# Moving one convolution pair of the input projection from the first part to the second, with its loads, scans and stores

## The chip, the cores and the metric

The kernel runs on one core of one Trainium2 chip. The metric is the device time of one execution in microseconds, the median over runs. The engines are TensorE (PE, with PEld for its weight loads), VectorE (DVE), ScalarE (ACT), GpSimd (POOL) and SyncE (SP). SP and POOL mostly issue DMAs here.

## What is computed

One layer of a decoder trunk on 1024 tokens of width 1024. The parts that matter, from the reference:

```python
h = rms_norm(x, g_mix[l])
z = jnp.einsum("bsd,de->bse", h, w_in[l]) + b_in[l]
va, ga, xb, gb, sa, sb = jnp.split(z, cuts, axis=-1)
u = va * jax.nn.sigmoid(ga)
u = causal_depthwise_conv(u, conv_a_w[l], conv_a_b[l])
...
v = causal_depthwise_conv(xb, conv_b_w[l], conv_b_b[l])
v = rg_lru(v, w_rg_a[l], b_rg_a[l], w_rg_x[l], b_rg_x[l], lam[l])
y_b = jnp.einsum("bsc,cd->bsd", v * jax.nn.gelu(gb), w_b_out[l])
```

After it come a layer norm, two more projections, gates, the output projection and an MLP, which the change doesn't touch. The projection `w_in` has 56 blocks of 128 columns: 8 of va, 8 of ga, 12 of xb, 12 of gb, 8 of sa and 8 of sb. A convolution over va times sigmoid(ga) has 31 taps; channel block j needs the column blocks VA + j and GA + j. `rg_lru` ends in a scan along the tokens.

## The kernel before

Matmuls take float32 operands as a high and a low part, each rounded for TensorE, and three products of these (high by high, high by low, low by high). A part is made in one of two ways: ScalarE copies the high part and VectorE subtracts it for the low one (`later(..., tensor_tensor, ..., ALU.subtract)`), or `split_dma` (L65 to L67) has ScalarE write the negated value, an accumulating DMA from POOL add the source, and ScalarE copy the high part.

**First part** (from L827, slots s = 3 to NC1 - 1, NC1 = 26). Each slot multiplies one column block of `w_in` (list `CH`) with all tokens: 24 pairs of operands times two halves, 48 matmuls (`chunk_mm`, L743). 16 head gates of `rg_lru` stand between, 12 matmuls each in two groups, the last at s = 22. The blocks are xb 0 to 11 and va, ga 0 to 6; the last two of `CH` are swapped. Beside it ScalarE and VectorE prepare the next weights (`w_parts`), gate the convolution input (`u_gate`, `u_mul`), and, three tiles at a time, run the scans: `scan_exp` (s = 22 for tiles 9 to 11), `scan_root` (s = 23, a square root with its own function table; it records a time `rooted[t]`), and `scan_tile` (L591), which takes a memset, three VectorE operations and a store of the tile to DRAM (`hd`, L597). Tile 9 goes in s = 23, tile 10 in s = 24, tile 11 in s = 25.

**Second part** (from L1038). The remaining 30 column blocks go in 15 pairs (`ZPAIRS`) by a seven-product scheme over 2 by 2 blocks (two columns by two halves of the rows; on the token side two token phases by the same halves). A product (i, p) is 12 matmuls (`z_mm`, L944). `zseq` orders them: pairs 0 and 1 are interleaved in 12 products, (0,1), (1,1), (0,2), (1,2), (0,6), (0,7), (1,7), (0,5), (1,6), (0,3), (0,4), (1,5), then seven for each pair. The left operand of product n + 4 is made in slot n (`z_lhs`, tile `zo`), sums of weight blocks it needs in slot n and n + 5 (`z_sums`, tile `zs`), and bank copies and results after the product (`z_post`, `z_post2`). Products p = 1, 2, 3 reuse the tokens of the first part; p = 6, 7, 5, 4 need differences of them, for each of two halves c2: `x_load` (L684) reads four tiles `xs` from DRAM, `x_sum` makes four differences on VectorE, and `x_parts` splits them into high and low (`xs6h`, `xs6l` and so on). The half c2 = 0 splits p = 5 and 4 by DMA, all others by VectorE. Each z product of p uses both halves.

A pair of gb columns is multiplied with the scan result (`z_h` loads `hd`, the product is stored to `hgd`); a pair with index below GA is a va, ga pair and goes to `z_u`, which makes the convolution input with a sigmoid; sa, sb pairs store gates. In the kernel before, pair 6 is va, ga 7.

**Order.** In these parts (`tc.manual_schedule`) ScalarE, VectorE, TensorE, SP and POOL run in the order of the code. VectorE's work of a slot is collected by `later(ready, cost, f, ...)` and emitted at the end of the slot by `vector_work`, sorted by `ready`, a time of the kernel's own cost clocks `clk`:

```python
    def vector_work(end):
        for ready, _, cost, f, a in sorted(todo, key=lambda x: x[:2]):
            dve(cost, ready, f, *a)
        todo.clear()
        taps["wait"] += fresh
        fresh.clear()
        fill(end)
```

`fill` puts taps of the convolutions (`conv`, L655, 47 operations each) where these clocks leave VectorE room. `ysum` collects the convolutions and is read by the layer norm after the second part. Most 128 by 1024 tiles come from one pool of 37 buffers (`T`). `z_load` (L761) brings a quarter of two pairs' weights into a pool "p" of 4 buffers, shared with the head inputs.

`XS` lists the token work by slot of the first part, `ZX` by product of the second. `x_load(1)` and the four `z_load`s of pairs 0 and 1 stand in slot NC1 - 3 = 23, in that order; `x_load(0)` in NC1 - 5 = 21.

Of the kernel before, what the change touches and what calls it, by code (L numbers as in the profile page):

```python
# [30 lines left out]
def trunk_kernel(ctx: ExitStack, tc: tile.TileContext, x, xt_in, xt_eo, vecs, w_in, w_a_out, w_b_pl, w_b_sq,  # L31
                 w_rg, w_o, w_1, w_2, g_final, out):

    nc = tc.nc
# [410 lines left out]
    VA, GA, XB, GB, SA, SB = 0, 8, 16, 28, 40, 48  # L445
# [72 lines left out]
    hd = dp.tile([12, P, S], F32, name="hd")  # L518
# [48 lines left out]
    at_, rooted = {}, {}  # L567
# [20 lines left out]
        for t in ts:  # L588
            later(ready, 1.2, nc.vector.tensor_tensor, gate[1, t], gate[1, t], vt.pop(t), ALU.mult)

    def scan_tile(t):  # L591
        a, r, i = at_.pop(t), gate.pop((0, t)), gate.pop((1, t))
        nc.vector.scalar_tensor_tensor(r, a, 1.0, r, ALU.add, ALU.mult)
        nc.vector.memset(r[:, 0:1], 1.0)
        nc.vector.tensor_tensor(i, r, i, ALU.mult)
        nc.vector.tensor_tensor_scan(i, a, i, 0.0, ALU.mult, ALU.add)  # L596
        nc.sync.dma_start(hd[t], i)  # L597

    ut = {}
    yd = dp.tile([8, P, S], F32, name="yd")  # L600
# [101 lines left out]
                      ALU.subtract)  # L702

    CH = [XB, VA, GA, XB + 1, XB + 2, VA + 1, GA + 1, XB + 3, XB + 4, XB + 5, VA + 2, GA + 2]
    CH += [XB + t for t in range(6, 12)] + [c for j in range(3, 7) for c in (VA + j, GA + j)]
    NU = 7
    CH[-2:] = CH[:-3:-1]
    NC1 = len(CH)
    zps = {n: z0[n] for n in range(N0)}
# [3 lines left out]
    def later(ready, cost, f, *a):  # L713

        todo.append((ready, len(todo), cost, f, a))
# [18 lines left out]
    def chunk_mm(s, n0, n1, halves=(0, 1)):  # L734

        wh, wl = wst[s]
        if s not in zps:
            zps[s] = PS(f"z{s}")
        pairs = [x for k in range(8) for x in ((wh, k, 0), (wh, k, 1))] + [(wl, k, 0) for k in range(8)]
        for n in range(n0, n1):  # L740
            w, k, part = pairs[n]
            for hf in halves:
                nc.tensor.matmul(zps[s][:, HALVES[hf]], w[:, k, :], xw[k][part][hf],  # L743
                                 start=n == 0, stop=n == 23)
        at("P", len(halves) * (n1 - n0) * MM)

    ZPAIRS = [GB + 2 * i for i in range(6)] + [VA + 7] + [SA + 2 * i for i in range(4)]
    ZPAIRS += [SB + 2 * i for i in range(4)]
    NZ = len(ZPAIRS)
    zraw, zs, zo, zb = {}, {}, {}, {}  # L750
    zn = [0]

    def z_load(i, kk):

        zraw[i, kk] = raw = qp.tile([P, 2, 4, P], F32, tag="p", name=f"zw{i}_{kk}", bufs=4)
        c = ZPAIRS[i]
        if c < GA:
            for m_, col in enumerate((GA + c, VA + c)):
                nc.sync.dma_start(raw[:, m_], w_in[col, :, 4 * kk:4 * kk + 4, :])
            return  # L760
        nc.sync.dma_start(raw, w_in[c:c + 2, :, 4 * kk:4 * kk + 4, :].rearrange("m p k c -> p m k c"))  # L761
# [47 lines left out]
    def z_get(n, f):  # L809
# [5 lines left out]
    head_at = {s: n for n, s in enumerate(HS0)}  # L815

    EXP = {head_slot: g for g, head_slot in enumerate(HS0[4 * g + 3] + 1 for g in range(4))}
    XS = {NC1 - 5: ((x_load, 0),), NC1 - 4: ((x_sum, 0),), NC1 - 3: ((x_load, 1), (x_parts, 0, 6)),
          NC1 - 2: ((x_sum, 1), (x_parts, 0, 7, 5)), NC1 - 1: ((x_parts, 0, 4), (x_parts, 1, 6))}
    made = []  # L820
    head_w(0)
    w_load(3)
# [4 lines left out]
    with tc.manual_schedule(engines=ENGINES):  # L827
        for s in range(3, NC1):
            w_load(s + 2)
            for t in sorted(vp_):  # L830
                head_load(t)
            taps["hold"] = False
            begun = clk["P"]
            clk["A"], clk["V"] = max(clk["A"], begun + 0.5), max(clk["V"], begun - 2)

            if s == 3:

                chunk_mm(s, 0, 24, (1,))
                rs = first_scale()
                first_product(0, rs)  # L840
                xb_out(0, zps[0])
                first_parts(rs)
                chunk_mm(s, 0, 24, (0,))
            else:
                mid = 16 if s - 1 in EXP else 12
                chunk_mm(s, 0, mid)
            before, new, nxt = (head_at.get(s + d) for d in (-1, 0, 1))
            if before is not None:

                head_gate(before, 0, begun)  # L850
                head_mm(before, 1)
            if made:
                xb_parts(made.pop())
            if s > 3:
                chunk_mm(s, mid, 24)
            if new is not None:
                head_mm(new, 0)

            c = CH[s - 1]
            if c >= XB:  # L860
                xb_out(c - XB, zps[s - 1])
            elif c >= GA:
                if CH[s] == c - GA + VA:
                    u_gate(c - GA, zps[s - 1])
                else:
                    u_out(c - GA, zps[s - 2], zps[s - 1])
            w_parts(s + 1)
            if before is not None:
                head_gate(before, 1, clk["P"] - (2 * (24 - mid) + 6) * MM)
            if s - 1 in EXP:  # L870

                scan_root(EXP[s - 1])
            if s == 3 or c >= XB:
                made.append(0 if s == 3 else c - XB)
            if nxt is not None:
                head_w_parts(nxt)
            if s in (5, 6):
                decay_on(27 if s == 5 else 99)
            if s + 2 in head_at:
                head_w(head_at[s + 2])  # L880

            def parts_now():
                if new is None and made:
                    vector_work(0)
                    xb_parts(made.pop())

            for d in range(5):
                if s - d in EXP:
                    g = EXP[s - d]
                    if d == 0:  # L890
                        scan_exp(g, parts_now)
                    if d == int(g < 3):
                        scan_in(begun if d else clk["P"] - 2, 3 * g, 3 * g + 1, 3 * g + 2)

                    t = 3 * g + d - (2 if g < 3 else 1)
                    if 3 * g <= t < 3 * g + 3:
                        later(rooted[t], 4.8, scan_tile, t)
            if s == NC1 - 1:
                z_get(0, z_lhs)
                z_get(1, z_lhs)  # L900
            for f, *a in XS.get(s, ()):
                f(*a)
            if s == NC1 - 3:
                for i in range(4):
                    z_load(i // 2, i % 2)
            if s == 3:
                for c2 in range(4):
                    nc.sync.dma_start(xu[0, c2], xc[c2])
            vector_work(clk["P"] - 0.7)
# [64 lines left out]
    def z_out(i, m_, hf, src, name):  # L974
        if ZPAIRS[i] < GA:
            z_u(i, ZPAIRS[i] - VA, m_, hf, src)
            return
        ci = ZPAIRS[i] + m_
        bias = bin_c[:, ci:ci + 1]
# [53 lines left out]
        elif p == 4:  # L1033
            z_out(i, 1, 0, zb[i, "u"], "c")

    ZX = {0: ((x_parts, 1, 7),), 2: ((x_parts, 1, 5),), 4: ((x_parts, 1, 4),)}
    H_AT = {2: (0, 0), 5: (1, 1), 3: (0, 1), 4: (1, 0)}
    with tc.manual_schedule(engines=ENGINES):  # L1038

# [154 lines left out]
        z_get(3, z_lhs)  # L1194
        u_mul(NU - 1, zps[NC1 - 1])
        vector_work(clk["V"])
        z_h(0, 0, 0)
        for n in range(len(zseq) + 2):
# [9 lines left out]
            if n + 3 < len(zseq):  # L1208
                i, p = zseq[n + 3]
# [760 lines left out]
    with tc.manual_schedule(engines={mybir.EngineType.Activation, mybir.EngineType.DVE,  # L1970
                                     mybir.EngineType.PE}):
        for n in range(len(useq)):
# [4 lines left out]
            while ready < min(len(useq), n + look + 1):  # L1977
                i, p = useq[ready]
# [316 lines left out]
```

## Time and profile before

| | |
|---|---|
| median of 3 runs | 1528.36 us (1528.01 to 1529.28) |
| profiled execution, its own time | 1528.49 us |
| span of its instructions | 1526.7 us |
| busy: PE, PEld | 1517.1 us (99%), 1248.3 us (82%) |
| busy: DVE, ACT, POOL | 1200.7 us (79%), 928.1 us (61%), 190.7 us (12%) |
| DMA | 295.48 MB, mean 194 GB/s |
| first part ends, second part begins | 338.56 us |
| `z` matmuls of L743 | 3 x 368 recorded |

Times in the views count from the first instruction of the profiled execution. A timeline row reads: start, duration, engine, line, operation, output <- inputs with buffer numbers left out, count; in brackets the idle time of the engine before it and what it waited for. Two rows that follow each other overlap by about 0.1 us where an engine is pipelined, so the distance of their starts is the price of the first. A table of stretches reads: length, then busy time and count of PE, PEld, DVE, ACT and POOL, the granted clock of TensorE, the DMA share and GB/s. A matmul record is longer (about 0.39 us) than the distance of two matmuls, since they are pipelined.

### The profile page before, as it was taken

How to read it: one execution, taken by the hardware profiler on the slowest of the kernel's cores; microseconds unless marked ns; L12 is line 12 of the kernel's file. 1: busy time of each engine (PE TensorE's matmuls, PEld its weight loads, DVE VectorE, ACT ScalarE, POOL GpSimd, SP SyncE). 2: the span in 40 equal slices, each digit the busy share in tenths (PEclk: the TensorE clock that was granted, in tenths of full speed). 3: DMA queues.
4: the chain of work that ended last, by engine and by line, in shares of the span. 5: the costliest groups of instructions: out<-in, count | busy, mean ns of one | idle time of the engine just before them, and what ended most of it. 6: DMA issues, size and time to landing. Idle time of an engine off the chain costs nothing.

```text
span 1526.7 us, 18955 instructions
## 1 busy us (share of the span) xinstructions
PE 1517.1 (99%) x6712; PEld 1248.3 (82%) x6712; DVE 1200.7 (79%) x1640; ACT 928.1 (61%) x1299; POOL 190.7 (12%) x228
## 2 busy tenths in 40 slices
PE   9999999999999999999999999999999999999998
PEld 7878887888888888888888888888888888888886
DVE  6999996999999997788769879755555387777777
ACT  6748688576566667645475777554444455545475
POOL 0111011022222222000022322000000000101010
PEclk9999999999999999999999999999999999999999
DMA  8757778698997789964779897333333974776464
GB/s 352 192 135 165 178 179 187 199 262 211 266 254 179 182 207 277 304 216 120 268 197 302 191 213 174 124 127 111 111 111 111 308 264 125 181 206 171 106 124 152
DMA packets 130911, 295.48 MB, mean 194 GB/s; under 512 B 12800, under 2 KB 34944, under 8 KB 130816
## 3 DMA queue, kind: packets, MB, share of 16 engines
q1 hardware_dynamic: 98960, 214.83, 41.5%
q0 software_dynamic: 31568, 78.92, 27.4%
q8 instruction: 52, 0.85, 0.2%
q10 hardware_dynamic: 288, 0.52, 0.1%
q14 instruction: 43, 0.35, 0.1%
HBM read 148.74 MB, written 60.82 MB: 137 GB/s over the span
## 4 chain that ended last, share of the span: by engine, by line
PE 99%; DMA 0%; DVE 0%; ACT 0%; SPq 0%; issue 0%
PE z L743 16%; PE d2b L2015 2%; PE d1b L2015 2%; PE d0b L2015 2%; PE z L273 2%; PE d3b L2015 2%; PE d0e L2015 1%; PE d3e L2015 1%; PE d3a L2015 1%; PE d2e L2015 1%; PE d1e L2015 1%; PE d1a L2015 1%; PE d0a L2015 1%; PE d2a L2015 1%; PE rg L550 1%; PE rg L552 1%
## 5 line engine op out<-in xcount | busy, mean ns | idle before, releaser
L743 PE MATMUL z<-xh,win_h 128*128 128x512 f32 x368 | 115.4, 391 | 0.0
L743 PE MATMUL z<-xl,win_h 128*128 128x512 f32 x368 | 114.9, 390 | 0.0
L655 DVE SCALAR_TENSOR_TENSOR y<-u,vec,y 128x511 f32<-128x511 f32 (+14 forms) x120 | 88.7, 739 | 0.0
L743 PE MATMUL z<-xh,win_l 128*128 128x512 f32 x368 | 87.5, 389 | 0.0
L655 DVE SCALAR_TENSOR_TENSOR yt<-u,vec,yt 128x511 f32<-128x511 f32 (+6 forms) x112 | 82.9, 740 | 0.0
L655 DVE SCALAR_TENSOR_TENSOR y<-yt,csum,y 128x511 f32<-128x511 f32 (+6 forms) x112 | 82.9, 740 | 0.0
L743 PEld LDWEIGHTS z<-xh,win_h 128*128 128x128 f32 x368 | 69.1, 188 | 16.0 <-ACT win_h L67 0.4
L743 PEld LDWEIGHTS z<-xl,win_h 128*128 128x128 f32 x368 | 69.1, 188 | 14.9
L743 PEld LDWEIGHTS z<-xh,win_l 128*128 128x128 f32 x368 | 69.1, 188 | 14.6
L560 ACT ACTIVATE g<-rg,vec 96x1024 f32<-96x1024 f32 x32 | 35.5, 1111 | 72.7 <-PE rg L552 72.7
L1710 ACT ACTIVATE o<-s 128x512 fp32r<-128x512 f32 x56 | 33.8, 624 | 45.2 <-DVE s L1694 26.4
L66 POOL DMA_DIRECT2D zo<-zw x45 | 38.9, 864 | 133.7 <-ACT zo L65 118.4
L501 DVE SCALAR_TENSOR_TENSOR v<-xb,vec,v 128x1023 f32<-128x1023 f32 (+2 forms) x36 | 46.2, 1282 | 4.4 <-ACT v L492 3.5
L66 POOL DMA_DIRECT2D db_10l<-br x4 | 3.5, 868 | 338.3 <-DMA br<-in_w_dram 253.1
L66 POOL DMA_DIRECT2D win_l<-win_raw x23 | 19.8, 861 | 190.6 <-ACT win_l L65 161.9
L65 ACT ACTIVATE zo<-zw 128x512 fp32r<-128x512 f32 x45 | 28.2, 627 | 24.3 <-PE z10f L944 2.1
L1234 DVE TENSOR_TENSOR o<-s,o 128x512 fp32r<-128x512 f32 x56 | 37.3, 684 | 1.5 <-ACT o L1710 1.5
L66 POOL DMA_DIRECT2D zo<-zs x30 | 26.1, 871 | 75.8 <-ACT zo L65 63.8
L67 ACT ACTIVATE zo<-zw 128x512 fp32r<-128x512 f32 x45 | 28.0, 622 | 0.0
L596 DVE TENSOR_TENSOR_SCAN g<-a,g 128x1024 f32<-128x1024 f32 x12 | 27.5, 2292 | 0.4
L66 POOL DMA_DIRECT2D ga<-gsa x8 | 6.9, 866 | 161.2 <-DMA m<-mbd 150.9
L1234 DVE TENSOR_TENSOR o<-w_raw,o 128x512 fp32r<-128x512 f32 x38 | 25.9, 685 | 0.0
(3178 smaller groups left out, 4908.2 us busy)
## 6 DMA issues: line engine op xcount, KB each, us to landing
w_raw<-in_w_dram SPq DMA_DIRECT2D x32, 512.0 KB, 5.5
br<-in_w_dram SPq DMA_DIRECT2D x32, 512.0 KB, 5.6
ar<-fd SPq DMA_DIRECT2D x32, 512.0 KB, 6.9
zw<-in_w_in_dram SPq DMA_DIRECT2D x28, 512.0 KB, 6.9
win_raw<-in_w_in_dram SPq DMA_DIRECT2D x23, 512.0 KB, 4.8
win_l<-win_raw POOLq DMA_DIRECT2D x23, 512.0 KB, 5.1
zo<-zw POOLq DMA_DIRECT2D x45, 256.0 KB, 5.7
gates<-zg SPq DMA_DIRECT2D x32, 256.0 KB, 4.5
```

The costliest lines, as they stand in the source:

```text
L65: nc.scalar.activation(l, src, AF.Copy, scale=-1.0)
L66: nc.gpsimd.dma_start(l, src, accum_op=ALU.add)
L67: nc.scalar.activation(h, src, AF.Copy)
L273: nc.tensor.matmul(z0[i][:, HALVES[hf]], w0[i][w][:, k, :], xpart(a, hf, k), start=k == 0 and which == "hh", stop=k == 7 and which == ("hl ...
L501: nc.vector.scalar_tensor_tensor(v[:, d:S], a[:, 0:S - d], cbw_c[:, w * 12 + t:w * 12 + t + 1], v[:, d:S], ALU.mult, ALU.add)
L560: nc.scalar.activation(a, gps.pop((n, gi))[:HD, :], AF.Sigmoid, bias=(ba_c, bx_c)[gi][:, n:n + 1])
L596: nc.vector.tensor_tensor_scan(i, a, i, 0.0, ALU.mult, ALU.add)
L655: nc.vector.scalar_tensor_tensor(o[:, k:], a[:, 0:HS - k], c, o[:, k:], ALU.mult, add)
L743: nc.tensor.matmul(zps[s][:, HALVES[hf]], w[:, k, :], xw[k][part][hf], start=n == 0, stop=n == 23)
L1234: tt(l, src, h.bitcast(F32), ALU.subtract)
L1710: nc.scalar.activation(o[:, 0], src, AF.Copy)
L2015: nc.tensor.matmul(o, a, b, start=start and n == 0, stop=stop and n == len(todo) - 1, skip_group_check=not start or not stop)
```

## The change

The va, ga pair 6 leaves `CH` (24 blocks, NC1 = 24) and becomes pair 4 of the second part, which has 16 pairs: gb 0 to 7, va and ga 6, gb 8 to 11, va and ga 7, then sa and sb. Slots counted from the end now mean other numbers:

| work | before | after |
|---|---|---|
| `x_load(0)`, `x_sum(0)` | s = 21, 22 | s = 21, 22 |
| `x_load(1)` | s = 23, ahead of the weights | s = 23, behind the weights |
| weights of pair 0 | s = 23 | s = 22 |
| weights of pair 1 | s = 23 | s = 23, after the matmuls in the code |
| left operands (0,1), (1,1) | s = 25 | s = 23, behind `scan_root` |
| `x_parts(0, ...)`: 6; 7; 5; 4 | s = 23; 24; 24; 25 | s = 23; 23; product 1; product 3 |
| `x_sum(1)` | s = 24 | product 0 |
| `x_parts(1, ...)`: 6; 7; 5; 4 | s = 25; product 0; 2; 4 | product 0; 1; 2; 4 |
| scan tiles 9; 10; 11 | s = 23; 24; 25 | s = 23; product 2; product 3 |
| store of scan tiles 10; 11 | with the scan | product 6; product 8 |

`scan_later` queues a scan with the `ready` time `rooted[t]` that `scan_root` recorded in s = 23. In s = 23 `u_gate` now belongs to the last convolution of the first part (j = 5), and there is no next weight to split.

```diff
-    def scan_tile(t):
+    scanned = {}
+
+    def scan_tile(t, late=False):
...
-        nc.sync.dma_start(hd[t], i)
+        if late:
+            scanned[t] = i
+        else:
+            nc.sync.dma_start(hd[t], i)
+
+    def scan_store(t):
+        nc.sync.dma_start(hd[t], scanned.pop(t))
+
+    def scan_later(t):
+        later(rooted[t], 4.8, scan_tile, t, True)
...
-    CH += [XB + t for t in range(6, 12)] + [c for j in range(3, 7) for c in (VA + j, GA + j)]
-    NU = 7
+    CH += [XB + t for t in range(6, 12)] + [c for j in range(3, 6) for c in (VA + j, GA + j)]
+    NU = 6
...
-    ZPAIRS = [GB + 2 * i for i in range(6)] + [VA + 7] + [SA + 2 * i for i in range(4)]
+    ZPAIRS = [GB + 2 * i for i in range(4)] + [VA + 6] + [GB + 8, GB + 10, VA + 7]
+    ZPAIRS += [SA + 2 * i for i in range(4)]
...
-    XS = {NC1 - 5: ((x_load, 0),), NC1 - 4: ((x_sum, 0),), NC1 - 3: ((x_load, 1), (x_parts, 0, 6)),
-          NC1 - 2: ((x_sum, 1), (x_parts, 0, 7, 5)), NC1 - 1: ((x_parts, 0, 4), (x_parts, 1, 6))}
+    XS = {NC1 - 3: ((x_load, 0),), NC1 - 2: ((x_sum, 0),), NC1 - 1: ((x_load, 1), (x_parts, 0, 6, 7))}
...
+            if s == NC1 - 1:
+                z_load(1, 0)
+                z_load(1, 1)
...
+            if s == NC1 - 2:
+                z_load(0, 0)
+                z_load(0, 1)
...
-            if s == NC1 - 3:
-                for i in range(4):
-                    z_load(i // 2, i % 2)
...
-    ZX = {0: ((x_parts, 1, 7),), 2: ((x_parts, 1, 5),), 4: ((x_parts, 1, 4),)}
+    ZX = {0: ((x_sum, 1), (x_parts, 1, 6)), 1: ((x_parts, 1, 7), (x_parts, 0, 5)), 2: ((scan_later, 10), (x_parts, 1, 5)), 3: ((x_parts, 0, 4), (scan_later, 11)), 6: ((scan_store, 10),), 8: ((scan_store, 11),),
+          4: ((x_parts, 1, 4),)}
```

## The prediction

> **What bounds the kernel now.** I read the core's span and clock first, then the waits of TensorE, then the busy time of the engines in the place that the change touches.
>
> ```profile
> core 0: 1526.7 us, clock 0.999
> ```
> ```profile
> PE z L273 <- ACT xh L235: 1.3, 1, 1.3
> PE spare L360 <- POOL ones L108: 1.0, 1, 1.0
> ```
>
> These two rows are the whole view of TensorE's waits (who waited, for whom, total us, times, longest). TensorE waits 2.3 us in 1526.7, both at the very start, so the span is the sum of its matmuls. Any added wait lands in the time in full, unless fewer matmuls pay for it.
>
> ```profile
> 316.80:338.56 21.76, 21.76 (x97) 18.02 (x96) 21.37 (x18) 15.69 (x20) 6.04 (x7) 1.00 0.91 234
> 338.56:357.60 19.04, 19.04 (x85) 15.77 (x84) 18.56 (x27) 13.66 (x21) 3.48 (x4) 1.00 0.81 214
> ```
> ```profile
> 338.56 0.39 PE L944 MATMUL z0a<-xh,zo 128*128 128x512 f32 x1
> ...
> 341.28 0.39 PE L944 MATMUL z1a<-xh,zo 128*128 128x512 f32 x1
> ```
>
> The last row pair is TensorE's timeline: the second part begins at 338.56, and its first product of 12 matmuls takes 341.28 - 338.56 = 2.72 us, 0.227 a matmul. A slot of the first part is 48 matmuls without gate matmuls, 4 x 2.72 = 10.88 us, so the last two slots are 316.80 to 338.56. The table of stretches gives for these two slots, and for the next seven products, the time, then the busy time of PE, PEld, DVE, ACT and POOL. The reader is to see the fourth figure: VectorE is busy 21.37 of 21.76 us and then 18.56 of 19.04. TensorE is bound, but VectorE runs beside it with no room at exactly this place.
>
> **The change part by part.** *Matmuls.* Two slots go, 2 x 48 = 96 matmuls; one more pair comes to the second part, 7 x 12 = 84. That is 12 fewer: -2.72 us. This is the only certain gain. The first part now ends at 316.80 instead of 338.56, and its slots up to there (s = 22 ends at 316.80 - 10.88 = 305.92) hold the same work, so the rows up to about 309 stay valid in absolute time.
>
> *ScalarE in the last slot (s = 23).*
>
> ```profile
> 309.77 1.04 ACT L65 ACTIVATE win_l<-win_raw 128x1024 fp32r<-128x1024 f32 x1
> 310.72 1.05 ACT L67 ACTIVATE win_h<-win_raw 128x1024 fp32r<-128x1024 f32 x1
> 311.79 1.28 ACT L584 ACT_TABLE_LOAD   x1
> 313.08 2.96 ACT L584 ACTIVATE g<-g 128x1024 f32<-128x1024 f32 x3
> 315.94 1.04 ACT L700 ACTIVATE xs6h<-xs 128x1024 fp32r<-128x1024 f32 x1
> 319.19 1.28 ACT L605 ACT_TABLE_LOAD   x1 [2.20 <-DVE g L596]
> 320.49 1.12 ACT L605 ACTIVATE u<-z,vec 128x1024 f32<-128x1024 f32 x1
> ...
> 330.71 0.62 ACT L65 ACTIVATE zo<-zw 128x512 fp32r<-128x512 f32 x1
> ```
>
> Today s = 23 splits the weights of the next slot (309.77 to 311.79, 2.02 us), then takes the three roots of the scans (table load, 313.08 to 316.04). After the change there is no next slot; the gate of the last convolution stands there, with a table load: 320.49 + 1.12 - 319.19 = 2.42 us. So the roots come 0.40 later and end at 316.44. Only then come the first two left operands of the second part (z_lhs). Today these stand at 330.71, almost 8 us ahead of their use at 338.56; after the change at 316.44, with TensorE due at 316.80.
>
> ```profile
> 331.63 0.86 POOL L66 DMA_DIRECT2D zo<-zw  x1 [3.68 <-ACT zo L65]
> ```
> ```profile
> DMA to landing us min/median/max: 3.2/6.7/7.8
> ```
>
> The low half of such an operand is a copy (0.62) and then an accumulating DMA, which POOL starts 331.63 - 331.33 = 0.30 us after the copy; the second row is how long these took to land in the stretch 300 to 345. So the first low half lands at 316.44 + 0.62 + 0.30 + 6.7 = 324.1 (320.6 to 325.2), and TensorE wants it at its third matmul, 316.80 + 0.45 = 317.25. That is a **first wait of 6.8 us** (3.3 to 7.9).
>
> *VectorE.* The scans of tiles 10 and 11, the four differences of the second half of the tokens (x_sum) and its first low part (xs6l) lay in the two slots that go. They now stand in the first four products, in one in-order queue with the low halves that TensorE waits for.
>
> ```profile
> 314.17 1.23 DVE L593 SCALAR_TENSOR_TENSOR g<-a,g 128x1024 f32<-128x1024 f32 x1 [0.76 <-ACT g L584]
> ...
> 319.03 1.20 DVE L480 TENSOR_TENSOR xs6l<-xs,xs6h 128x1024 fp32r<-128x1024 f32 x1
> 320.15 4.99 DVE L480 TENSOR_TENSOR xs<-xs,xs 128x1024 f32<-128x1024 f32 x4
> ...
> 338.17 0.69 DVE L480 TENSOR_TENSOR zs<-zw,zw 128x512 f32<-128x512 f32 x1
> 338.89 0.69 DVE L480 TENSOR_TENSOR zs<-zs,zw 128x512 f32<-128x512 f32 x1
> 339.50 0.69 DVE L480 TENSOR_TENSOR zs<-zw 128x512 f32<-128x512 f32 x1
> 340.10 1.28 DVE L480 SCALAR_TENSOR_TENSOR u<-z,vec,u 128x1024 f32<-128x1024 f32 x1
> 341.75 1.23 DVE L480 TENSOR_TENSOR xs7l<-xs,xs7h 128x1024 fp32r<-128x1024 f32 x1 [0.37 <-ACT xs7h L700]
> 342.90 0.69 DVE L480 TENSOR_TENSOR zs<-zw 128x512 f32<-128x512 f32 x1
> 343.50 0.69 DVE L480 TENSOR_TENSOR zo<-zs,zo 128x512 fp32r<-128x512 f32 x1
> ...
> 346.74 1.22 DVE L480 TENSOR_TENSOR xs5l<-xs,xs5h 128x1024 fp32r<-128x1024 f32 x1
> 347.87 0.68 DVE L480 TENSOR_TENSOR zs<-zw,zw 128x512 f32<-128x512 f32 x1
> 348.59 0.69 DVE L480 TENSOR_TENSOR zs<-zs,zw 128x512 f32<-128x512 f32 x1
> 349.20 0.69 DVE L987 TENSOR_TENSOR hb<-hb,ze 128x512 f32<-128x512 f32 x1
> 349.80 0.68 DVE L480 TENSOR_TENSOR zo<-zs,zo 128x512 fp32r<-128x512 f32 x1
> ```
>
> Prices are start to start. One scan tile: 319.03 - 314.17 = 4.86. The operand to watch is the low half of product (0, 5), the eighth product (n = 7): it is made on VectorE in slot n = 3, and there the scan of tile 11 is sorted ahead of it, since its ready time (rooted) is from s = 23. Today it is written at 349.80 + 0.68 = 350.48 and wanted at 338.56 + 19.04 + 0.45 = 358.05: a slack of 7.6 us.
>
> After the change scan 9 begins 0.40 later, at 314.57, and ends at 319.43. Then, in code order: xs6l and xs7l of the first half, 1.12 + 1.15; three weight sums, 1.93; u, 1.28; x_sum of the second half, 4.99; its xs6l, 1.12; a sum and the low half of (0, 7), 0.60 + 0.69; xs7l, 1.15; a sum, 0.60; **scan 10, 4.86**; the low half of (1, 7), 0.69; xs5l, 1.13; two sums, 1.33; **scan 11, 4.86**; the product hb, 0.60; the low half of (0, 5), 0.68. Together 28.78 us: written at 348.21. TensorE wants it at 316.80 + 19.04 + 0.45 = 336.29. **The delay is 11.92 us**, and the first wait of 6.8 is part of it, not added: VectorE's queue waits for nothing that TensorE's wait moves. The other operands of these seven products come earlier by the same count (xs6l of the second half at 331.0, wanted by product 5 at 329.3, or 336.1 behind the first wait; the low half of (1, 7) at 339.6, wanted at 333.6, or 340.4).
>
> *ScalarE in the second part* gets xs6 of the second half and xs5 and xs4 of the first, some 5 us in slots 0 to 3. It waits for x_sum until about 329 and is behind by then. From there to the copy that product (0, 5) writes onto stand eight copies of 1.0, ten short operations of 0.6 and a table load of 1.28, some 15 us: due near 344, ahead of the 348.2, so nothing beyond. Sigmoids between GELUs in pair 4 add table loads of 1.28 each, four; the same change of functions stands in today's pair 6, with no wait in the list above: 0. If that cover failed, one load would be the price.
>
> *Loads and stores.* SP now issues the four weight loads around the token loads, which go behind them; both kinds (4 MB) start before 310 as today, and x_sum needs its data only at 324.9: 0, and with the cover gone the landing's excess. The scan stores move behind slots 6 and 8, their readers are pair 6: 0. The gate tile u of s = 23 needs a buffer of the common pool; today it waited 2.20 us for one (row 319.19). The bounds are 0, and 2.20 moved onto the roots and so onto all of VectorE's queue; I take 0, since the tiles of today's holders xs6 come after it now.
>
> *Convolution taps.* They fill VectorE's gaps and are pushed back by what the scans and x_sum (9.72 + 4.99) now take in the second part.
>
> ```profile
> L668 POOL DMA_DIRECT2D ysum<-y x7: 862/1212/1416, 178.2 to 586.5; - x7
> ...
> L1251 ACT ACTIVATE mu1h<-ysum x1: 615/615/615, 638.7 to 638.7; 128x512 fp32r<-128x512 f32 x1
> ```
>
> The last sum of convolutions is issued at 586.5 and read at 638.7; 52 us cover the 15 and the new pair's few us: 0. Late taps also hold buffers that the third part wants; bounds 0 to 3 us, the longest wait of that kind today being the 2.20.
>
> Sum against the profiled execution: -2.72 + 11.92 = +9.20; 1528.49 + 9.20 = 1537.69. That execution stands 0.13 over the median 1528.36, so I say **1537.6**.
>
> **The rivals.** *The cover holds (not slower).* Operands are made four products ahead, and today's slack at (0, 5) is 7.6 us. Moved work below that would cost nothing and only -2.72 would remain: 1525.6. It decides at 7.6 us; I count 7.6 + 11.92 = 19.5 moved ahead of that operand. For it speaks only that the queue might run in another order than the code's.
>
> *Only the first wait.* If the two scans came behind the low halves of their slots, 9.72 leaves the queue, the delay there is 2.2, and the first wait of 6.8 decides: 1528.4 + 6.8 - 2.7 = 1532.5 (1529.0 to 1533.6 by the landings). Against it: the queue is sorted by ready times, and the roots are old.
>
> *The clock drops after the wait.* Before (0, 5) TensorE would stand still for 11.92 - 6.8 = 5.1 us. Today's rows show a clock of 0.999 and no stop over 1.3 us, so they can't tell. Were the ten matmuls left of product (0, 5) taken at half pace, 10 x 0.227 = 2.3 us more: 1539.9; only this second wait counts, since the first is inside the 11.92. The Trainium skill, page "TensorE: Matmul & The Clock Gate", section "Part 1: The HAM clock gate", has such a rule: a window of about 3.4 us without work halves the clock, and a busy window of that length brings it back. By its figure, an estimate, it would be 1.7 us. No row of this trace agrees or disagrees.
>
> *More waits behind it.* Buffer waits, late taps, or low halves of products 9 and 10 landing up to 1.1 later than the median (7.8 against 6.7): 3.5 to 8 us more, 1541 to 1546.
>
> **How the numbers follow.** Forecast 0.57, clock 0.15, more waits 0.15, only the first wait 0.08, cover 0.05. A measurement tells about 0.2%, 3.1 us, from no change. The cover's -2.7 is within it or just past it (0.03 and 0.02), and the low end of the first wait alone is within it (0.02): faster 0.02, same 0.05, slower 0.93. The range 1534 to 1543 holds the forecast with 3.6 us less, the clock, and the lower part of more waits.
>
> **What would show it.** TensorE's waits must list two new ones: for a low half by DMA at 317, some 3 to 8 us, and for VectorE's zo from about 343, about 5. VectorE's timeline must show scans at about 334 and 342 with no gap of note from 314 to 348. Slot 22 must end at 305.9. The forecast is wrong if VectorE's order has the low halves ahead of the scans, or if TensorE's waits sum to under 8 us.

## The result, and the profile after

| | before | after |
|---|---|---|
| median | 1528.44 us (1528.01 to 1529.28, 4 runs) | 1544.53 us (1542.28 to 1546.59, 4 runs) |
| ratio | | 1.0104, 95% interval 1.0087 to 1.0122 |
| profiled execution, its own time | 1528.49 us | 1542.28 us |
| span | 1526.7 us | 1540.5 us |

The change costs 16.1 us. The forecast was 1537.6 with a range up to 1543.0, so the median lies 1.5 us above the range. Lines are those of the changed kernel: L958 is the z matmul (L944 before), L595 to L598 a scan tile (L593 to L596), L1001 the addition into hb (L987), L1024 and L1027 the copies between PSUM banks, L679 the transfer that adds a convolution to ysum (L668).

First the span and the clock of the core, then TensorE's whole list of waits. Before, the list had two rows and 2.3 us.

```profile
core 0: 1540.5 us, clock 0.996
```
```profile
PE z0a L958 <- DMA zo<-zw: 3.0, 1, 3.0
PE z0e L958 <- DVE zo L480: 2.7, 1, 2.7
PE z0e L958 <- ACT z0e L1027: 1.5, 1, 1.5
PE spare L360 <- POOL ones L108: 1.0, 1, 1.0
PE z14f L958 <- DMA zo<-zw: 1.0, 1, 1.0
PE z3e L958 <- DMA zo<-zs: 0.7, 1, 0.7
PE z0a L958 <- ACT zo L67: 0.7, 1, 0.7
PE z L273 <- ACT xh L235: 0.5, 1, 0.5
PE z6e L958 <- DMA zo<-zs: 0.5, 1, 0.5
PE z15e L958 <- DMA zo<-zs: 0.2, 1, 0.2
```

Three groups are new: the first product (z0a, 3.7 us), the product (0,5) (z0e, 4.2 us), and four late products that the forecast's sum didn't have (z3e, z6e, z14f, z15e, 2.4 us). The waits don't add up to the loss: TensorE was also slower behind them. The table of stretches has the last two slots of the first part, then the second part up to product (1,6), then seven more products.

```profile
294.79:316.55 21.76, 21.76 (x97) 17.62 (x95) 17.95 (x21) 18.73 (x18) 0.86 (x1) 1.00 0.81 250
316.55:351.37 34.82, 26.96 (x98) 20.90 (x97) 34.01 (x36) 24.82 (x37) 8.61 (x10) 0.85 0.73 169
351.37:370.40 19.03, 19.03 (x85) 15.78 (x84) 7.85 (x12) 11.78 (x21) 4.31 (x5) 1.00 1.03 299
```

In the middle stretch VectorE is busy 34.01 of 34.82 us: it sets the pace. The clock there is 0.85. Right behind it VectorE has 7.85 us of work in 19.03. So VectorE has room in the second part, but not in its first eight products.

TensorE's timeline at the two stops:

```profile
317.40 0.50 PE L958 MATMUL z0a<-xh,zo 128*128 128x512 f32 x1 [0.69 <-ACT zo L67]
...
321.12 1.22 PE L958 MATMUL z0a<-xh,zo 128*128 128x512 f32 x2 [2.98 <-DMA zo<-zw]
...
344.13 0.50 PE L958 MATMUL z0e<-xs5h,zo 128*128 128x512 f32 x1 [1.50 <-ACT z0e L1027]
...
347.55 1.22 PE L958 MATMUL z0e<-xs5h,zo 128*128 128x512 f32 x2 [2.68 <-DVE zo L480]
348.57 0.63 PE L958 MATMUL z0e<-xs5l,zo 128*128 128x512 f32 x1
...
351.37 0.39 PE L958 MATMUL z1b<-xs6h,zo 128*128 128x512 f32 x1
...
637.88 0.39 PE L1159 MATMUL yb0b<-hb1h,wba0h 128*128 128x512 f32 x1
```

Without stops the second part would start at 316.55, the third matmul of (0,5) would run at 316.55 + 19.04 + 0.45 = 336.04, and (1,6) would start at 316.55 + 8 x 2.72 = 338.31. They run at 347.55 and 351.37: 11.51 and 13.06 us late. The 1.55 us between these two delays is the slow pace: the last ten matmuls of (0,5) take 351.37 - 347.55 = 3.82 us in place of 10 x 0.227 = 2.27.

VectorE's timeline, for the forecast's queue:

```profile
324.43 5.07 DVE L480 TENSOR_TENSOR xs<-xs,xs 128x1024 f32<-128x1024 f32 x4
...
333.49 1.22 DVE L595 SCALAR_TENSOR_TENSOR g<-a,g 128x1024 f32<-128x1024 f32 x1
...
341.38 1.22 DVE L595 SCALAR_TENSOR_TENSOR g<-a,g 128x1024 f32<-128x1024 f32 x1
...
344.02 2.29 DVE L598 TENSOR_TENSOR_SCAN g<-a,g 128x1024 f32<-128x1024 f32 x1
346.23 0.67 DVE L1001 TENSOR_TENSOR hb<-hb,ze 128x512 f32<-128x512 f32 x1
346.81 0.68 DVE L480 TENSOR_TENSOR zo<-zs,zo 128x512 fp32r<-128x512 f32 x1
```

None of these rows has a bracket, nor have those left out: VectorE waits for nothing. Scans 10 and 11 stand at 333.49 and 341.38, and the low half of (0,5), the last row, is written at 346.81 + 0.68 = 347.49, when TensorE's third matmul goes on.

The late waits. First POOL's timeline at one of them, then the profile's summary of issues in the stretch 402 to 416 (KB each, median us from issue to landing):

```profile
402.48 1.23 POOL L679 DMA_DIRECT2D ysum<-y  x1
405.27 0.87 POOL L66 DMA_DIRECT2D zo<-zs  x1 [1.57 <-ACT zo L65]
```
```profile
ysum<-y POOLq DMA_DIRECT2D x1, 512.0 KB, 11.3
...
zo<-zs POOLq DMA_DIRECT2D x1, 256.0 KB, 10.0
```

A finished convolution is added to ysum by a transfer of 512 KB from POOL, and the low half of (3,3) is issued 2.8 us behind it on the same queue. It takes 10.0 us to land, at 415.3, and TensorE waits for it (z3e). In the stretch 300 to 345 the median of such low halves was 5.1, but there the DMA share was lower (0.76, against 1.03 from 402 to 416); what the sum itself adds is read below, from the run without the sums. The same order stands ahead of z6e (issued at 463.43, 2.8 us behind a sum, landed after 9.7 us) and of z14f (611.22, 0.7 us behind, 10.1 us). The wait at z15e is another case: its low half was issued at 625.63, 15 us behind the last sum, and landed in 7.1 us. It was issued late, since ScalarE had waited 4.29 us for VectorE, and VectorE 5.84 us ahead of that.

The books of the profiled execution, at the start of the third part (yb0b): before 624.20, after 637.88, so +13.68. Worked out: -2.72 for 12 matmuls fewer, -0.25 since the second part was due at 316.55 and not 316.80 (single executions differ that much: in e6_order_alone below it began at 338.23, not 338.56), +11.51 for the operand of (0,5), +1.55 for the pace behind it, and, from the starts of the products, +1.04, +0.81, +1.28 and +0.51 = +3.64 at the four late ones. That is +13.73.

### The profile page after: what moved, and what is told of

The parts are those of the page before. It is cut to its first block, busy times and chain, and to the rows that moved or that the text cites. A ratio compares the mean times of both kernels' runs of the same rounds, so it can differ in the third digit from the quotient of the medians.

```text
span 1540.5 us, 18986 instructions
## 1 busy us (share of the span) xinstructions
PE 1521.4 (99%) x6700; PEld 1249.8 (81%) x6700; DVE 1205.3 (78%) x1649; ACT 937.4 (61%) x1316; POOL 192.6 (13%) x231
## 4 chain that ended last, share of the span: by engine, by line
PE 93%; DMA 3%; issue 1%; DVE 1%; ACT 1%; SPq 0%; POOL 0%; DVEq 0%; POOLq 0%; ACTq 0%
PE z L754 14%; PE d2b L2030 2%; PE d1b L2030 2%; PE d0b L2030 2%; PE z L273 2%; DMA zo<-zs 2%; PE d3b L2030 2%; PE d0a L2030 1%; PE d0e L2030 1%; PE d2a L2030 1%; PE d3e L2030 1%; PE d3a L2030 1%; PE d2e L2030 1%; PE d1e L2030 1%; PE d1a L2030 1%
## 5 line engine op out<-in xcount | busy, mean ns | idle before, releaser
L754 PE MATMUL z<-xh,win_h 128*128 128x512 f32 x336 | 105.6, 392 | 0.0
L754 PE MATMUL z<-xl,win_h 128*128 128x512 f32 x336 | 105.1, 390 | 0.0
L754 PE MATMUL z<-xh,win_l 128*128 128x512 f32 x336 | 79.9, 390 | 0.0
L754 PEld LDWEIGHTS z<-xh,win_h 128*128 128x128 f32 x336 | 63.1, 188 | 14.7 <-ACT win_h L67 0.4
L754 PEld LDWEIGHTS z<-xl,win_h 128*128 128x128 f32 x336 | 63.1, 188 | 13.6
L754 PEld LDWEIGHTS z<-xh,win_l 128*128 128x128 f32 x336 | 63.1, 188 | 13.3
L65 ACT ACTIVATE zo<-zw 128x512 fp32r<-128x512 f32 x48 | 30.0, 625 | 26.2 <-PE z11f L958 2.1
L67 ACT ACTIVATE zo<-zw 128x512 fp32r<-128x512 f32 x48 | 29.8, 620 | 0.0
L598 DVE TENSOR_TENSOR_SCAN g<-a,g 128x1024 f32<-128x1024 f32 x12 | 27.5, 2290 | 0.4
```

The lines of the kernel that those rows point to most:

```text
L65: nc.scalar.activation(l, src, AF.Copy, scale=-1.0)
L67: nc.scalar.activation(h, src, AF.Copy)
```

## The experiments

Theory, after this reading: four separate delays. VectorE's queue at the head of the second part (11.5 us, the scans above all), the clock behind the stop (1.55), the sums of the convolutions issued ahead of left operands (3.6 in this execution), and a first wait that hides inside the first of these. Rivals: the new pair itself costs (its sigmoids between GELUs, its table loads); or ScalarE, not VectorE, is the late one. Numbers are medians; the kernel before stood at 1528.22 to 1528.37 beside them.

**The new order of pairs alone (e6_order_alone).** The kernel before, with its va, ga pair as pair 4.

```diff
-    ZPAIRS = [GB + 2 * i for i in range(6)] + [VA + 7] + [SA + 2 * i for i in range(4)]
+    ZPAIRS = [GB + 2 * i for i in range(4)] + [VA + 7] + [GB + 8, GB + 10]
+    ZPAIRS += [SA + 2 * i for i in range(4)]
```

> The kernel before with the va, ga pair 7 as pair 4 between gb pairs and nothing else, so the four table loads stand where the change has them. Theory (table loads are covered): no new wait of TensorE for ScalarE, 1528.4 within 0.5 us, unless a sum of a convolution falls on another operand (up to 1.3 us each). Rival (table loads make operands late): waits in pairs 4 and 5, 1 to 3 us more.

Measured 1528.56 (1528.10 to 1529.17), ratio 1.0001 (0.9992 to 1.0010). No new wait stands in the list. The order of pairs and its table loads cost nothing. The added pair wasn't run by itself, but the books above leave nothing for it.

**The moved work alone (e5_work_alone).** The kernel before, with its 26 slots and 15 pairs, and in it x_sum(1), the late pieces and scans 10 and 11 where the change has them.

```diff
-          NC1 - 2: ((x_sum, 1), (x_parts, 0, 7, 5)), NC1 - 1: ((x_parts, 0, 4), (x_parts, 1, 6))}
+          NC1 - 2: ((x_parts, 0, 7),)}
-                    if 3 * g <= t < 3 * g + 3:
+                    if 3 * g <= t < 3 * g + 3 and t < 10:
-    ZX = {0: ((x_parts, 1, 7),), 2: ((x_parts, 1, 5),), 4: ((x_parts, 1, 4),)}
+    ZX = {0: ((x_sum, 1), (x_parts, 1, 6)), 1: ((x_parts, 1, 7), (x_parts, 0, 5)),
+          2: ((scan_later, 10), (x_parts, 1, 5)), 3: ((x_parts, 0, 4), (scan_later, 11)),
+          4: ((x_parts, 1, 4),), 6: ((scan_store, 10),), 8: ((scan_store, 11),)}
```

> The kernel before with its 26 slots and 15 pairs, but the second half's differences, the later token parts and scans 10 and 11 stand in the second part as in the change (weights and first left operands stay early). Theory (the moved VectorE work makes the second wait, the pair itself only takes the cover): from 338.2 the queue up to the low half of (0, 5) is 26.5 us, so it is written at 364.7 and wanted at 358.05; a wait of some 6.6 us, about 1.5 us of slow matmuls behind it, no wait at the first product; 1536 to 1541 with late waits of 0 to 4 us. Rival (the moved pair costs the time): within 1 us of 1528.4.

Measured 1539.39 (1538.49 to 1542.26), ratio 1.0078 (1.0062 to 1.0093): moving the work costs 11 us without any new pair. But the stop isn't where it was expected. TensorE's list:

```profile
PE z1a L954 <- ACT z1b L1020: 6.0, 1, 6.0
...
PE z0e L954 <- DVE zo L480: 0.2, 1, 0.2
```

Here ScalarE's copy of a bank is late, and the wait at (0,5) is 0.2 us. ScalarE itself had waited 7.00 us for a weight sum of VectorE, 2.26 for the token differences and 2.67 for a buffer that a sum of the convolutions held. The weight sum was late because 19 convolution taps had taken VectorE's room from 326.49 to 338.85, where the kernel before ran scans 10 and 11. So the total agreed with the expectation by luck: the place of the stop was another.

**Which part of the work (e11_scans_alone, e12_loads_alone).** Each moves one part: the two scans (with pieces (0,4) and (1,6) in slots 3 and 0, since the scan tiles hold their buffers), or the sum and pieces of the tokens.

The scans alone, with XS without its last slot and the scans held back as above:

```diff
-    ZX = {0: ((x_parts, 1, 7),), 2: ((x_parts, 1, 5),), 4: ((x_parts, 1, 4),)}
+    ZX = {0: ((x_parts, 1, 6),), 1: ((x_parts, 1, 7),), 2: ((scan_later, 10), (x_parts, 1, 5)),
+          3: ((x_parts, 0, 4), (scan_later, 11)), 4: ((x_parts, 1, 4),), 6: ((scan_store, 10),), 8: ((scan_store, 11),)}
```

> The kernel before with the order of its loads and sums kept and scans 10 and 11 alone moved into the second part, at the places that the change gives them (with them, two of the last operand pieces of the first block, which have no buffers otherwise, given out in slots 0 and 3). Theory (VectorE's queue at the head of the second part adds up, and the two scans are some 10 us of the 29): 1532 to 1537, with a wait of 3 to 8 us at the products (0,5) to (1,7), so the scans are the larger part of the 11 us that all moved work cost. Rival (the sums and loads that come late are the larger part): 1528 to 1531.

The tokens alone, with XS as in the run of the moved work and the scans where they were:

```diff
-    ZX = {0: ((x_parts, 1, 7),), 2: ((x_parts, 1, 5),), 4: ((x_parts, 1, 4),)}
+    ZX = {0: ((x_sum, 1), (x_parts, 1, 6)), 1: ((x_parts, 1, 7), (x_parts, 0, 5)), 2: ((x_parts, 1, 5),),
+          3: ((x_parts, 0, 4),), 4: ((x_parts, 1, 4),)}
```

> The kernel before with scans 10 and 11 left in the first part, and only the second token sum and the operand pieces behind it moved into the second part as in the run that moved all work. Theory (the scans are the larger part): 1528.5 to 1532.5, with waits of at most 3 us in all among the first twelve products. Rival: 1534 to 1538, with a wait of 4 us or more on ScalarE or on a token load there.

Measured 1536.47 (1535.48 to 1538.42), ratio 1.0054 (1.0042 to 1.0067) for the scans, and 1529.91 (1529.12 to 1530.62), ratio 1.0012 (1.0003 to 1.0021) for the tokens. So 8.2 and 1.7 of the 11 us that both cost together. The scans are the larger part. VectorE's timeline of the first of these kernels shows how:

```profile
341.33 0.73 DVE L666 SCALAR_TENSOR_TENSOR y<-u,vec,y 128x498 f32<-128x498 f32 x1
341.98 0.69 DVE L480 TENSOR_TENSOR zs<-zw,zw 128x512 f32<-128x512 f32 x1
```

Where scan 11 ran from 332.21 before the change, 15 convolution taps run here, from 332.21 to 341.98: `fill` gave the room away. The weight sum zs comes at 341.98, not 338.17, ScalarE waits 7.0 us for it, and TensorE 2.3 for the bank copy behind it. The scans then come on top, at 349.83 and 357.71. So part of the 8.2 us is the taps that took the scans' place, as in the run of all moved work; the changed kernel has no taps there, and how the 8.2 divide isn't settled.

**Scans behind the operands of their slot (e1_scans_behind).** The ready time is moved so that the sorted queue has the scans last, in slots 3 and 5; stores at 8 and 10.

```diff
-        later(rooted[t], 4.8, scan_tile, t, True)
+        later(clk["A"] + 3, 4.8, scan_tile, t, True)
```

> Scans 10 and 11 stand behind the low half of product (0, 5) in VectorE's queue (slots 3 and 5, last of their slot; stores at products 8 and 10); all else as in the change. Theory (VectorE's queue sets the second wait, the first wait is inside it): TensorE's second wait, 4.2 us in two rows of the change, and the slow matmuls behind it go; the first wait of 3.0 + 0.7 us and its slow matmuls, 6.9 us in all, stay. Product (1, 6) begins at about 345.2 instead of 351.37. Time about 6 us under the change, near 1538. Rival (the second wait is ScalarE's or a buffer's, not the scans'): the waits at z0e stay, time within 1 us of the change, near 1544.

Measured 1548.56 (1547.15 to 1549.95), ratio 1.0135 (1.0119 to 1.0150): 4.0 us slower than the change, where 6 us faster was expected. VectorE, ScalarE and TensorE of this kernel:

```profile
337.63 0.68 DVE L480 TENSOR_TENSOR zo<-zs,zo 128x512 fp32r<-128x512 f32 x1
```
```profile
340.87 1.06 ACT L67 ACTIVATE xs4h<-xs 128x1024 fp32r<-128x1024 f32 x1 [3.31 <-DVE g L597]
...
344.84 0.58 ACT L1027 ACTIVATE z0e<-z0b 128x512 f32<-128x512 f32 x1
```
```profile
PE z0e L958 <- ACT z0e L1027: 3.8, 1, 3.8
PE z0e L958 <- DMA zo<-zs: 3.0, 1, 3.0
```

The low half of (0,5) is 9.2 us earlier than after the change. But ScalarE's xs4h needs one of the 37 buffers, the scan of tile 10 frees it, and behind xs4h stands the copy onto which (0,5) accumulates: 344.84, where the changed kernel had 343.50. The product had two guards, VectorE's queue and, through the buffers, ScalarE's. Taking one away shows the other, and (1,6) begins at 349.92, only 1.5 us earlier. The loss comes behind it: product (0,3) stops 3.05 us for a low half that took 9.5 us to land, 3.2 after the change, and with its slow pace costs 4.8 us. Why that one landed so late isn't shown.

**The first operands ahead of the roots (e2_lhs_first), and the first weights loaded earlier (e9_early_loads).**

```diff
+            if s == NC1 - 1:
+                z_get(0, z_lhs)
+                z_get(1, z_lhs)
             if s - 1 in EXP:
                 scan_root(EXP[s - 1])
...
-            if s == NC1 - 1:
-                z_get(0, z_lhs)
-                z_get(1, z_lhs)
```

> The first two left operands are made ahead of the square roots in slot 23; nothing else differs from the change. Theory (the first wait is inside the second): the first wait falls from 3.0 to under 1 us, but the roots and with them scan 9 and VectorE's whole queue come 2.1 us later, so the low half of (0, 5) is written at about 349.6 instead of 347.5 and product (1, 6) begins 1 to 3 us later than 351.37; time 1544 to 1547, not faster. Rival (the waits add up): time 4 to 6 us under the change, 1538 to 1540.

```diff
-            if s == NC1 - 2:
+            if s == NC1 - 3:
                 z_load(0, 0)
                 z_load(0, 1)
```

> The changed kernel with one edit: the two token loads of pair 0 in the second part are given out one slot of the first part earlier, so that 1 MB less is in flight when the first low half of that part is sent. Theory (the first wait of TensorE, 3.0 us plus the half pace behind it, is a transfer that shares the DMA engines with the loads): the low half lands within about 4 us of its issue, where it took 4.0 to 7 us before, and the first wait falls from 3.0 to under 1.5 us. The total hardly moves, 1542 to 1545, because the wait for the low half of (0,5) takes up what the first one gives. Rival (it is ScalarE's or VectorE's queue that is late): the first wait stays at 2.7 to 3.2 us, total the same.

(What the second text calls token loads are the two weight loads of pair 0.) Measured 1547.70 (1545.33 to 1548.31), ratio 1.0123 (1.0109 to 1.0137), and 1546.26 (1543.64 to 1547.78), ratio 1.0111 (1.0095 to 1.0126). Against 3.0 us after the change the wait for the low half was 2.9 and 3.8 us, so neither cure worked alone; the rival of the first text, that the waits add up, is out too. In the first, POOL issued the low half 3.1 us earlier and TensorE went on at the same time as after the change (321.12):

```profile
314.04 0.86 POOL L66 DMA_DIRECT2D zo<-zw  x1 [15.11 <-ACT zo L65]
```
```profile
321.23 1.15 PE L958 MATMUL z0a<-xh,zo 128*128 128x512 f32 x2 [2.88 <-DMA zo<-zw]
```

In the second the issue was at 317.57 and TensorE went on at 322.39. Landings of 7.2 and 4.8 us, against 4.0 after the change: each edit alone gave back in the landing what it gained, or gained nothing. The last kernel below has both edits, and there the low half was issued at 314.74 and TensorE went on at 319.36, 4.6 us later. The run before that one (e8_best) has ScalarE's order alone, issued the low half at 314.76 and went on at 321.37, 6.6 us later. So, with the issue early, the place of pair 0's weights is worth 2.0 us of landing: ScalarE's order and the loads in flight both guard the first product. Why the loads moved alone gained nothing isn't shown.

**TensorE kept busy ahead of the stops (e3_fill).** 12 matmuls without use ahead of the first product and 14 ahead of (0,5).

```diff
+            if n in FILLS:
+                junk = zp.tile([P, HS], F32, tag="z", name=f"junk{n}")
+                for k in range(FILLS[n]):
+                    nc.tensor.matmul(junk, xbh[1][0][:, 0:P], xbh[1][0][:, HALVES[0]], start=True, stop=True)
             z_get(n, z_mm)
```

> TensorE gets 12 idle matmuls ahead of the first product of the second part and 14 ahead of product (0, 5), into a bank that nothing reads; operands of the real products come as before. If the matmuls behind the waits are slow because TensorE stood still (0.43 us apart instead of 0.227, twice in the change's profile), they keep 0.227 now and product (1, 6) begins at about 349.9 instead of 351.37: time 1.5 us under the change, near 1543, with less spread between runs than the 4.3 us of the change. Rival (the pace falls for another reason, such as operands that are written while they are read): the matmuls stay 0.43 apart and the time is the change's or longer by up to 1 us.

Measured 1544.37 (1543.62 to 1546.30), ratio 1.0106 (1.0092 to 1.0120), clock 0.999.

```profile
347.08 0.73 PE L958 MATMUL z0e<-xs5h,zo 128*128 128x512 f32 x2 [2.23 <-DVE zo L480]
347.65 0.39 PE L958 MATMUL z0e<-xs5l,zo 128*128 128x512 f32 x1
...
349.48 0.39 PE L958 MATMUL z1b<-xs6h,zo 128*128 128x512 f32 x1
```

The pace behind the stop is whole, and (1,6) starts at 349.48, 1.9 us before the 351.37 of the changed kernel. The slow pace came from the stops, then. In the total nothing is left of the gain: from the starts of the products the late waits were 6.4 us in this execution, where the changed kernel's had 3.6.

**Without the sums (e4_no_sum), and with the sums held back (e7_sums_held).**

```diff
-            nc.gpsimd.dma_start(ysum[0], acc, accum_op=add)
+            pass
```

> The sums of the convolutions over the channel blocks (the accumulating DMAs into ysum for blocks 1 to 7) are left out; the convolutions and their stores stay. Theory (the late waits at z3e, z6e, z14f and z15e come from left operands that queue behind such a DMA, since the taps now end at another phase of the products): these four waits, with their excess of 1.04 + 0.81 + 1.28 + 0.51 = 3.6 us, go; time about 3.4 us under the change, near 1541. Rival (they come from the pair order and its table loads on ScalarE): the waits stay, time within 1 us of the change.

```diff
-            nc.gpsimd.dma_start(ysum[0], acc, accum_op=add)
+            held_sums.append(acc)
...
             z_get(n + 4, z_lhs)
+            if n + 4 >= len(zseq) or zseq[n + 4][1] == 1:
+                sums_out()
```

> The change, but the accumulating DMA of a convolution into ysum is held back until the left operand of the next product p = 1 has been issued, behind which POOL has its longest gap (6 us). Nothing is left out. Theory (late operands queue behind that DMA): the late waits at z3e, z6e, z14f and z15e go or fall under 1 us in sum; 1540 to 1541, like the run without the sums. Rival (the sums cost by their traffic, wherever they stand): 1543 to 1546.

Measured 1539.83 (1538.38 to 1540.08), ratio 1.0072 (1.0059 to 1.0085) without the sums, and 1540.98 (1540.11 to 1543.79), ratio 1.0085 (1.0071 to 1.0099) with the sums behind the next (i,1) operand. In both all four late waits are gone; the two early stops stay. The low half of (3,3), which landed 10.0 us after its issue behind a sum, has this row without the sums:

```profile
zo<-zs POOLq DMA_DIRECT2D x1, 256.0 KB, 7.6
```

With the sums held it is 8.1. So a sum ahead adds some 2 us, and the rest of the 10.0 is that stretch's other traffic. It isn't POOL's queue alone: two transfers that SP issued in the same microsecond landed after 9.1 and 9.6 us beside the sum and after 5.6 and 7.2 without it. For z15e, VectorE's wait of 5.84 us is 3.80 without the sums and 1.30 with the sums held, and ScalarE's copy comes earlier with it.

The second kernel has one new row, at the end of the part. There the last sum is issued at 622.73, and ScalarE waits 2.16 us for a load; that the late sum delays this load is likely, not shown:

```profile
PE yb0b L1165 <- ACT yb0a L1185: 1.8, 1, 1.8
```

So the four late waits come from the sums at their new places, three through a low half issued right behind and one through VectorE. They are 4.7 us of the median; with the transfers kept and only their place changed, 3.6 us of it are back.

**All cures together (e8_best, e10_best2).** The first: sums held, scan 10 last in slot 3, scan 11 in slot 6, pieces (0,4) and (1,4) in 5 and 6, the last u gate behind the first operands. The second: scan 11 in slot 10, (1,4) left in 6, the weights of pair 0 earlier, and the sums of the last 20 products not held.

```diff
+    ZX = {0: ((x_sum, 1), (x_parts, 1, 6)), 1: ((x_parts, 1, 7), (x_parts, 0, 5)), 2: ((x_parts, 1, 5),),
+          3: ((scan_later, 10),), 5: ((x_parts, 0, 4),), 6: ((x_parts, 1, 4), (scan_later, 11)),
+          9: ((scan_store, 10),), 11: ((scan_store, 11),)}
```

> The change with the held sums, with scan 10 behind the low half of (0, 5) in slot 3, the p = 4 token parts in slots 5 and 6 (behind the buffers that scan 10 frees), scan 11 last in slot 6, its stores at 9 and 11, and the gate of convolution 5 behind the first left operands, so the roots and these operands come 2.4 us earlier. Theory: first wait 1 to 2 us, no wait for ScalarE's copy or VectorE at (0, 5) over 1 us, no late waits; 1527 to 1531. Rival (another operand is late in turn, as when the scans alone were moved): 1534 or more.

```diff
-          3: ((scan_later, 10),), 5: ((x_parts, 0, 4),), 6: ((x_parts, 1, 4), (scan_later, 11)),
-          9: ((scan_store, 10),), 11: ((scan_store, 11),)}
+          3: ((scan_later, 10),), 5: ((x_parts, 0, 4),), 6: ((x_parts, 1, 4),),
+          10: ((scan_store, 10), (scan_later, 11)), 14: ((scan_store, 11),)}
```

> The sums held back as in the run before it, scan 10 last in slot 3, scan 11 moved on to slot 10, the loads of pair 0 one slot earlier, the last u gate behind the first operands. Theory (five separate delays, each with its own cure: loads in flight, scans ahead of the low half of (0,5), scan 11 ahead of the sum that frees a PSUM bank, the sums' transfers, the half pace behind a stop): 1527 to 1531, with a first wait of 0 to 2 us and no other wait of more than 1 us until the end of the part. If it is 1525 to 1527, the pair's 2.7 us are got back. Rival (the moved work doesn't fit into the second part: VectorE and ScalarE are too full there, and each cure makes the next operand late): 1535 to 1539, with a new wait of 2 us or more at a later product.

Measured 1538.78 (1537.92 to 1539.64), ratio 1.0068 (1.0055 to 1.0081), and 1537.77 (1536.01 to 1538.92), ratio 1.0059 (1.0046 to 1.0071). Both missed the 1527 to 1531. In the first the stop at (0,5) is gone, and (0,4), three products later, stops instead:

```profile
354.15 0.80 PE L965 MATMUL z0f<-xs4h,zo 128*128 128x512 f32 x1 [3.41 <-DVE zc L480]
```

VectorE's addition that frees this PSUM bank stands behind scan 11. With scan 11 later still, the waits are many and small:

```profile
PE z0a L965 <- DMA zo<-zw: 2.2, 1, 2.2
PE z2a L965 <- DMA zo<-zw: 1.9, 1, 1.9
PE z15a L965 <- DMA zo<-zw: 1.4, 1, 1.4
PE z15e L965 <- ACT zc L1042: 1.2, 1, 1.2
...
PE z0f L965 <- DVE zc L480: 0.9, 1, 0.9
PE z1a L965 <- ACT z1b L1031: 0.6, 1, 0.6
```

With the stop at (0,5) gone, the first wait is no longer hidden inside it: 4.13 us and 2.5 of slow pace behind it in the first kernel, 2.16 and 1.8 in the second. The rival of the last text gave 1535 to 1539 by a new wait of 2 us or more at a later product; the time is in it, the longest new wait is 1.9. That each cure makes the next operand late is shown for scan 11; for the small waits of the last kernel it is only likely. No version here beats the kernel before. The gain to be had was 2.7 us, and the best version still lost 9.4.

## Why the prediction was right in its direction and too small

*The matmuls (-2.72).* Right: the books close to 0.05 us with it.

*VectorE's queue (+11.92).* Right, with 11.51 measured; the low half of (0,5) was forecast for 348.21 and written at 347.49, and the scans came at 333.49 and 341.38 where "about 334 and 342" was said. (The forecast says its prices are from start to start, but enters x_sum's recorded 4.99; from start to start it is 4.91, which changes nothing.) That the scans are the larger part of the moved work is borne out by the pair of runs, 8.2 against 1.7 us, with the taps named there. That VectorE alone guards (0,5) was not so: with its queue cleared, ScalarE's copy came at 344.84 by way of a buffer. The forecast costed that copy at "due near 344, ahead of the 348.2, so nothing beyond", which held for this kernel (343.50), but was no slack to speak of.

*The first wait (6.8, inside the 11.92).* Its place and its guard were right, its size not: 3.7 us, as the low half landed 4.0 us after its issue and not 6.7. It cost nothing in the sum, as forecast. The cause given, ScalarE's order, isn't the whole: earlier operands alone left the wait for the low half as it was (2.9), and earlier weights with them brought it to 2.2.

*The clock.* It was made a rival, with 2.3 us, when it should have been a term of the sum: the forecast itself had TensorE standing 5.1 us before the low half of (0,5). The measured stops there were 1.50 and 2.68, and the price 1.55.

*The step that failed: the convolution taps, costed at 0.* The forecast asked whether the last sum comes in time for its own reader, and that held: "52 us cover the 15 and the new pair's few us". It did not ask what lands beside the sums. Moved in time, three of them were issued 0.7 to 2.8 us ahead of low halves with little slack, and a fourth product was late by way of VectorE: +3.64 in the profiled execution, 4.7 in the median by the run without them. The rival "more waits behind it", 1541 to 1546 with a chance of 0.15, holds the measured time. It named late taps, buffers and landings up to 1.1 us later, but at other products (9 and 10); the landing at z3e was 10.0, 3.3 over the 6.7.

*Order of pairs, table loads, scan stores (0).* Right for the order and its loads (ratio 1.0001). The stores weren't tried by themselves; no wait in the list names one.

With these terms the forecast's 1537.69 becomes 1537.69 - 0.41 - 0.25 + 1.55 + 3.64 = 1542.22, against the profiled execution's 1542.28. The median lies 2.25 above that execution, the fastest of its four, while the forecast took 0.13 off for it, as the kernel before had it. These 2.25 us are not explained: the other runs of the changed kernel have no trace. Where the late waits exist, the profiled executions of the variants had 3.6 to 7.9 us of them, so they may be larger in the other runs; but the spread doesn't settle it, since the runs without the sums spread over 1.7 us, and those with the sums held, which have no late wait either, over 3.7, against 4.3 after the change.

## What to carry to other kernels

When work is moved into a full stretch of an in-order engine, add its whole duration to the operands queued behind it, then look for a second guard of the same product (buffers, banks, another engine's queue) before you call a reordering a cure. For a transfer that moves in time, ask not only whether its own reader still has slack but what is issued right behind it. A forecast that contains a stop of TensorE of several us must hold the slow pace behind it as a term of the sum, not as an alternative: in the second part of all kernels here, every stop of more than 2.3 us had it.

## What the runs showed of the hardware

Short stops are enough to slow TensorE. In the run with the scans alone, a stop of 2.28 us was followed by half pace (two matmuls in 0.85 us, where 0.45 is usual) for about 3.3 us:

```profile
346.06 0.50 PE L955 MATMUL z0a<-xh,zo 128*128 128x512 f32 x1 [2.28 <-ACT z0b L1021]
...
346.75 1.06 PE L955 MATMUL z0a<-xh,zo 128*128 128x512 f32 x2
347.60 0.63 PE L955 MATMUL z0a<-xl,zo 128*128 128x512 f32 x1
...
350.04 0.40 PE L955 MATMUL z0a<-xl,zo 128*128 128x512 f32 x1
```

In the filled kernel a stop of 2.23 us cost no pace at all, and in the last version, behind a stop of 2.16, matmuls ran at full pace until 320.9 and at half pace from there to 324.3. So the slow stretch of some 3.4 us doesn't begin with the stop's end. The Trainium skill, page "TensorE: Matmul & The Clock Gate", section "Part 1: The HAM clock gate", has a free-running window of about 3.4 us over which TensorE's activity is watched; the length and the late start agree with that. It asks for an idle window, though, and these stops were shorter than one; the measurement decides, and a stop of 2.2 us can be enough. Behind the first stop of the changed kernel the half pace lasted longer, from 321.12 to about 326.7.

An accumulating transfer of 512 KB makes what is issued just behind it land later: the 256 KB of (3,3) took 10.0 us 2.8 us behind a sum and 7.6 without the sums, those of (6,3) 9.7 and 7.3. How much of this is the order on POOL's queue and how much the sharing of the DMA engines isn't separated; SP's transfers beside it were slower as well.
